# Six columns of zeros beside three products of a group

## Chip, cores and metric

One core of a Trainium2 chip runs the whole program. The metric is the device time of one execution in microseconds.

## The reference

A decoder trunk of two layers works on 16 meta tokens and 256 tokens with 2048 features in float32. Layer 0 is forgetting attention, layer 1 is stick-breaking attention on keys and values that have a projection of their own; each layer ends in an MLP with squared ReLU. Shortened:

```python
h = concatenate([meta, x])                                  # 272 x 2048
for layer in range(2):
    a = rms_norm(h, norm_attn[layer])
    if layer == 0:
        q, k, v, f = split(a @ fox_w_in)
        h = h + forgetting_attention(q, k, v, cumsum(log_sigmoid(f + b_f))) @ fox_w_o
    else:
        k, v = split(rms_norm(h, kv_norm) @ w_kv)
        h = h + stick_breaking_attention(a @ sb_w_q, k, v) @ sb_w_o
    m = rms_norm(h, norm_mlp[layer])
    h = h + square(relu(m @ w_up[layer])) @ w_down[layer]
return rms_norm(h, final_norm)[16:]
```

Only the last 256 tokens are returned. So in layer 1 the queries, the output projection and the MLP are computed for 256 tokens, the keys and values for 272.

## The kernel before

Everything is kept with the features on the partitions: `hT` holds the residual stream as 16 chunks of 128 features by 272 tokens. A matrix product with 2048 x 512 weights is a **group** (`gemm_group`). It makes four accumulators `acc` in PSUM (m = 0 to 3, 128 output features each) and runs over four blocks of weights (kb = 0 to 3) with four chunks of 128 input features each (kc).

The products run in the type fp32r with operands that are split in two. ScalarE rounds a weight tile `raw` to `whi` (line 222), VectorE forms the remainder `wlo` (line 223), and the inputs are split likewise into `hi` and `lo` of a `Split` tile. For each weight tile and chunk there are three products: whi with hi, whi with lo, and wlo with hi. A group therefore has 4 x 4 x 4 x 3 = 192 products of a 128x128 weight tile with 272 columns (layer 0, and the keys and values) or 256 columns (the rest of layer 1, `t0` = M = 16). Each product has its own weight load on TensorE. All of them are issued by the helper `gemm_matmul`, so the profile puts them on line 175, and the name of the input tile tells the stage: x_a for the normed input of the query, key and value projections of layer 0 and of the queries of layer 1, x_kv for the shared keys and values, x_o for the output projections, x_m for the MLP's up, x_u for its down projections.

The order of a block's products is fixed by `series`. For 256 columns:

```python
series = [(w, x, kc, m) for w, x in ((0, "hi"), (0, "lo"), (1, "hi")) for m in ms for kc in kcs]
```

In the first block, `ms` is one accumulator and `kcs` is all four chunks, so the first twelve products of a group are whi with hi for the chunks 0 to 3, whi with lo for the chunks 0 to 3, and wlo with hi for the chunks 0 to 3, all into accumulator 0. `gemm_matmul` also ties each product to the one before, so that the scheduler keeps this order.

Layer 1 has, in this order, 4 groups of the query projection (the norm's `finish` comes inside the first one, with two plain fp32 products `pms_a`, line 156), 8 groups of keys and values with the attention's own work between them, 4 groups of the output projection (`out_proj`), and the MLP: four times four up and four down groups. Inside the first up group, ahead of the third block, stands `finish` again (`pms_m`).

The `Split` tiles come from a pool with two buffers. A tile has 16 rows of 640 elements for each partition; with 256 tokens, hi takes the elements 0 to 255 of a row and lo takes 320 to 575, so 64 elements behind each are unused. The tile `pad` (128x32 zeros, written by POOL at the start) is not read by anything.

Of the kernel before, what the change touches and what calls it, by code (L numbers as in the profile page):

```python
# [15 lines left out]
P = 128  # L16
D = 2048
NC = D // P
M = 16
# [5 lines left out]
N_FF = 4  # L25

ROWS = {0: (48, 368), M: (0, 320)}
XROW = 640

G_A0, G_M0, G_KV, G_A1, G_M1, G_FIN = range(6)  # L30
# [3 lines left out]
def yoco_kernel(ctx: ExitStack, tc: tile.TileContext, hT_in, gains, b_f, w_f, w_qkv0, w_o0, w_up, w_dn,  # L34
                w_kv, w_q1, w_o1, outT):
    nc = tc.nc
# [77 lines left out]
    pad = align.tile([P, 32], F32, name="pad")  # L114
# [3 lines left out]
    class Split:  # L118


        def __init__(self, label, t0):
            n = T - t0
            self.t0 = t0
            rows = xs.tile([P, NC * XROW + 64], F32R, tag="x", name=f"x_{label}")
            hi, lo = ROWS[t0]
            o = min(hi, lo)
            rows = rows[:, o:o + NC * XROW].rearrange("p (c t) -> p c t", c=NC)
            self.hi, self.lo = (rows[:, :, k - o:k - o + n] for k in (hi, lo))

    def split_chunk(sp, gi, c):  # L130

        g = g_sb[:, gi, c:c + 1]
        nc.scalar.activation(sp.hi[:, c], hT[:, c, sp.t0:], AF.Copy, scale=g)
        nc.vector.scalar_tensor_tensor(out=sp.lo[:, c], in0=hT[:, c, sp.t0:], scalar=g,
                                       in1=sp.hi[:, c].bitcast(F32), op0=ALU.mult, op1=ALU.subtract)
# [37 lines left out]
    def gemm_matmul(*args, **kw):  # L173

        ins = nc.tensor.matmul(*args, **kw).ins  # L175
        if queued and pinned[0]:
            tc.add_manual_dep(ins, queued[0].name, mybir.DependencyInfo(mybir.DependencyClass.NoSync,
                                                                        mybir.DependencyReason.DATA))
        queued[:] = [ins]

    def gemm_group(wblk, sp, t0, evac, before={}, after={}, load_x=None):

        uid[0] += 1
        u = uid[0]
        accs = [pacc.tile([P, 512], F32, tag="acc", name=f"acc_{u}_{m}") for m in range(4)]
        n = T - t0  # L190
        for kb in range(4):
            src_w = wblk[kb].rearrange("p (k c) -> p k c", k=4)
            if kb in before:
                before[kb]()
            piece = 1 if load_x is not None and kb < 2 else 2
            raws = [wraw.tile([P, 2, 512], F32, tag="raw", name=f"raw_{u}_{kb}_{hf}") for hf in range(2)]
            for k0 in range(0, 4, piece):
                if load_x is not None:
                    load_x(range(4 * kb + k0, 4 * kb + k0 + piece))
                if load_x is not None and kb == k0 == 0:  # L200

                    for c0 in (0, 256):
                        nc.scalar.dma_start(raws[0][:, 0, c0:c0 + 256], src_w[:, 0, c0:c0 + 256])
                else:
                    nc.sync.dma_start(raws[k0 // 2][:, k0 % 2:k0 % 2 + piece], src_w[:, k0:k0 + piece])
            parts = []
            for hf in range(2):
                whi = wspl.tile([P, 2 * 576], F32R, tag="whi", name=f"whi_{u}_{kb}_{hf}")
                wlo = wspl.tile([P, 2, 576], F32R, tag="wlo", name=f"wlo_{u}_{kb}_{hf}")
                if t0:  # L210
                    whi = whi.rearrange("p (k c) -> p k c", k=2)[:, :, 16:528]
                    wlo = wlo[:, :, 16:528]
                else:
                    whi = whi[:, :1024].rearrange("p (k c) -> p k c", k=2)
                    wlo = wlo[:, :, :512]
                boxes = [(o, piece, 0, 512) for o in range(0, 2, piece)]
                if load_x is not None and kb == hf == 0:
                    boxes[:1] = [(0, 1, 0, 256), (0, 1, 256, 512)]
                for o, no, c0, c1 in boxes:
                    src = raws[hf][:, o:o + no, c0:c1]  # L220
                    hp, lp = whi[:, o:o + no, c0:c1], wlo[:, o:o + no, c0:c1]
                    on_act = nc.scalar.activation(hp, src, AF.Copy)  # L222
                    on_dve = nc.vector.tensor_tensor(out=lp, in0=src, in1=hp.bitcast(F32), op=ALU.subtract)  # L223
                parts.append((whi, wlo))
            if kb in after:
                with tc.issue_after(on_act.ins), tc.issue_after(on_dve.ins):
                    after[kb]()


            if load_x is not None and kb == 0:  # L230
                runs = [([kc], range(4)) for kc in range(4)]
            elif kb in (0, 3):
                runs = [(range(4), [m]) for m in range(4)]
            else:
                runs = [(range(2 * hf, 2 * hf + 2), range(4)) for hf in range(2)]
            pinned[0] = load_x is None
            for kcs, ms in runs:
                if t0:
                    series = [(w, x, kc, m) for w, x in ((0, "hi"), (0, "lo"), (1, "hi")) for m in ms for kc in kcs]
                else:  # L240
                    series = [(w, x, kc, m) for m in ms for kc in kcs for w, x in ((0, "hi"), (0, "lo"), (1, "hi"))]
                for w, x, kc, m in series:
                    gemm_matmul(accs[m][:, :n], parts[kc // 2][w][:, kc % 2, m * P:(m + 1) * P],
                                getattr(sp, x)[:, 4 * kb + kc], start=kb == kc == w == 0 and x == "hi", stop=kb == kc == 3 and w == 1)
                if kb == 3:
                    for m in ms:
                        evac(m, accs[m][:, :n])
# [101 lines left out]
    ao = Split("o0", 0)  # L349
    for g in range(4):  # L350
# [11 lines left out]
        if g == 0:  # L362

            gemm_group(w_qkv0[0], xa, 0, lambda m, acc, qT=qT: nc.scalar.copy(qT[:, m, :], acc),
                       after={kb: (lambda kb=kb: first_norm(kb)) for kb in range(4)}, load_x=load_x)
# [11 lines left out]
        def decays(j):  # L377

            for i, (o, n) in enumerate(((0, 144), (144, T))):
# [5 lines left out]
                   after={j: (lambda j=j: decays(j)) for j in range(4)})  # L385
# [75 lines left out]
    def out_proj(w, ao, t0, gi, label):  # L461
        norm = Norm(label, t0)
        xm = Split(label, t0)
        for g in range(4):
            def evac(m, acc, g=g):
                c = 4 * g + m
                residual_add(c, acc, t0)
                split_chunk(xm, gi, c)
                norm.add(c)
            gemm_group(w[g], ao, t0, evac)  # L470
        return xm, norm

    def mlp(layer, xm, norm, t0, last_evac):
        box = {}

        def get_rstd():
            box["r"] = norm.finish()

        for f in range(N_FF):
            u = Split(f"u{layer}_{f}", t0)  # L480
            for g in range(4):
                def evac(m, acc, g=g):
                    c = 4 * g + m
                    r = tmp.tile([P, T], F32, tag="relu", name=f"relu_{layer}_{f}_{c}")
                    u2 = tmp.tile([P, T], F32, tag="u2", name=f"u2_{layer}_{f}_{c}")
                    nc.vector.scalar_tensor_tensor(out=r[:, t0:], in0=acc, scalar=0.0, in1=box["r"][:, t0:],
                                                   op0=ALU.max, op1=ALU.mult)
                    nc.scalar.activation(u2[:, t0:], r[:, t0:], AF.Square)
                    nc.scalar.activation(u.hi[:, c], u2[:, t0:], AF.Copy)
                    nc.vector.tensor_tensor(out=u.lo[:, c], in0=u2[:, t0:], in1=u.hi[:, c].bitcast(F32),  # L490
                                            op=ALU.subtract)
                gemm_group(w_up[layer, f, g], xm, t0, evac, {2: get_rstd} if f == g == 0 else {})
            for g in range(4):
                def evac(m, acc, g=g):
                    residual_add(4 * g + m, acc, t0)
                    if f == N_FF - 1:
                        last_evac(4 * g + m)
                gemm_group(w_dn[layer, f, g], u, t0, evac)

    xm, norm_m = out_proj(w_o0, ao, 0, G_M0, "m0")  # L500


# [16 lines left out]
    for g in range(4):  # L519
        def evac_q1(m, acc, g=g):  # L520
            q = qT1[g][:, m, :S]
            nc.vector.scalar_tensor_tensor(out=q, in0=acc, scalar=QSCALE, in1=box["rstd"][:, M:],
                                           op0=ALU.mult, op1=ALU.mult)
        def split_c(kb, g=g):
            for c in ([4 * kb + g - 1] if g < 3 else [4 * kb + 2, 4 * kb + 3]):
                split_chunk(xc, G_KV, c)

        gemm_group(w_q1[g], xq, M, evac_q1, {2: get_rstd1} if g == 0 else {},
                   after={kb: (lambda kb=kb: split_c(kb)) for kb in range(4)} if g else {})

    ao = Split("o1", M)
    for g in range(4):
# [80 lines left out]
    xm, norm_m = out_proj(w_o1, ao, M, G_M1, "m1")  # L613
# [36 lines left out]
    for i in range(2):  # L650
        pr = patt.tile([P, 512], F32, tag="patt", name=f"pr_fin_{i}")
        for b in range(2):
            nc.tensor.matmul(pr[:, b * P:(b + 1) * P], rs[:, b:b + 1].to_broadcast([P, P]), ident,
                             start=True, stop=True)
# [67 lines left out]
```

## Time and profile before

| what | value |
|---|---|
| median of three runs | 2330.26 us (2329.82 to 2330.46) |
| the profiled execution | 2329.83 us |
| its span, first to last instruction | 2328.0 us |
| TensorE busy | 2316.8 us |
| VectorE, ScalarE busy | 1289.9 us, 1040.6 us |
| POOL busy | 38.4 us |
| read from HBM | 407.29 MB |

PE is TensorE's products, PEld its weight loads, DVE is VectorE, ACT is ScalarE, POOL is GpSimd, and SP issues most DMAs. TensorE's products are pipelined: one is listed with more than twice the time after which the next one starts. So its busy time and the mean time of one product don't tell the rate; a stretch's length over its count of products does. A row of groups reads: line, engine, operation, tile written <- tiles read, shape, count | busy us, mean ns of one | idle time before them and who ended it. A piece of the chain that ended last reads: start in us, length in us, engine, tile, line, count.

### The profile page before, as it was taken

The numbers are of one execution on the slowest core, as the hardware profiler recorded it, in microseconds if no ns is written. First come the engines' busy times: TensorE is split into PE (matmuls) and PEld (weight loads), VectorE is DVE, ScalarE is ACT, GpSimd is POOL, SyncE is SP. The second block draws the span as 40 slices with busy tenths as digits, with TensorE's granted clock in tenths as the row PEclk, the third lists the DMA queues.
The fourth block names the chain that finished last, engine by engine and source line by source line (L and its number), as shares of the span: only waits on it lengthen the run. The fifth ranks groups of instructions, "written<-read, shape, count | busy, mean of one in ns | idle before, by whom it ended". The sixth has DMA issues, their size and how long they took to land.

```text
span 2328.0 us, 44800 instructions
## 1 busy us (share of the span) xinstructions
PE 2316.8 (100%) x19030; PEld 2309.8 (99%) x19030; DVE 1289.9 (55%) x1764; ACT 1040.6 (45%) x1397; POOL 38.4 (2%) x58
## 2 busy tenths in 40 slices
PE   9999999999999999999999999999999999999998
PEld 9999999999999999999999999999999999999998
DVE  7656556554455455455565555566555555555554
ACT  6444344443353344344544444455534434443553
POOL 1000000000000000000000000000000000000000
PEclk9999999999999999999999999999999999999999
DMA  7444545555555555555555444456565655656563
GB/s 240 166 163 157 181 154 168 185 174 180 181 170 185 172 184 177 183 170 184 173 188 183 156 153 149 152 180 199 180 192 178 194 182 184 195 182 191 179 192 127
DMA packets 116904, 412.32 MB, mean 177 GB/s; under 512 B 13520, under 2 KB 16992, under 8 KB 116704
## 3 DMA queue, kind: packets, MB, share of 16 engines
q1 hardware_dynamic: 114560, 406.29, 53.7%
q8 instruction: 149, 2.44, 0.4%
q10 hardware_dynamic: 2144, 3.17, 0.4%
q14 instruction: 51, 0.42, 0.1%
HBM read 407.29 MB, written 2.11 MB: 176 GB/s over the span
## 4 chain that ended last, share of the span: by engine, by line
PE 99%; DVE 0%; DMA 0%; ACT 0%; SPq 0%; issue 0%; DVEq 0%; ACTq 0%
PE acc L175 96%; PE ps L392 0%; PE pv L325 0%; PE pza L569 0%; PE po L454 0%; PE po L608 0%; DMA raw<-w_qkv 0%; PE po L609 0%; PE pzb L570 0%; PE po L455 0%; DVE ob L664 0%; PE pf L291 0%; PE pf L292 0%; PE pta L584 0%; PE pta L585 0%; PE pp L424 0%
## 5 line engine op out<-in xcount | busy, mean ns | idle before, releaser
L223 DVE TENSOR_TENSOR wlo<-raw,whi 128x1024 fp32r<-128x1024 f32 (+1 forms) x773 | 928.7, 1217 | 761.5 <-ACT whi L222 759.8
L222 ACT ACTIVATE whi<-raw 128x1024 fp32r<-128x1024 f32 (+1 forms) x773 | 796.5, 1049 | 1034.2 <-PE acc L175 1006.5
L175 PE MATMUL acc<-x_u,whi 128*128 128x272 f32 (+1 forms) x4096 | 651.9, 284 | 0.0
L175 PE MATMUL acc<-x_m,whi 128*128 128x272 f32 (+1 forms) x4096 | 651.7, 284 | 0.0
L175 PEld LDWEIGHTS acc<-x_u,whi 128*128 128x128 f32 x4096 | 573.9, 189 | 0.0
L175 PEld LDWEIGHTS acc<-x_m,whi 128*128 128x128 f32 x4096 | 573.6, 189 | 0.1
L175 PE MATMUL acc<-x_u,wlo 128*128 128x272 f32 (+1 forms) x2048 | 445.3, 284 | 0.0
L175 PE MATMUL acc<-x_m,wlo 128*128 128x272 f32 (+1 forms) x2048 | 445.2, 284 | 0.0
L175 PE MATMUL acc<-x_a,whi 128*128 128x272 f32 (+1 forms) x2048 | 361.8, 289 | 0.1
L175 PEld LDWEIGHTS acc<-x_u,wlo 128*128 128x128 f32 x2048 | 327.6, 189 | 0.0
L175 PEld LDWEIGHTS acc<-x_m,wlo 128*128 128x128 f32 x2048 | 327.5, 189 | 0.0
L175 PEld LDWEIGHTS acc<-x_a,whi 128*128 128x128 f32 x2048 | 303.4, 189 | 1.4 <-ACT whi L222 0.4
L175 PE MATMUL acc<-x_a,wlo 128*128 128x272 f32 (+1 forms) x1024 | 254.8, 287 | 0.0
L175 PE MATMUL acc<-x_kv,whi 128*128 128x272 f32 x1024 | 191.8, 288 | 0.0
L175 PEld LDWEIGHTS acc<-x_a,wlo 128*128 128x128 f32 x1024 | 176.5, 189 | 0.9 <-issue 0.5
L175 PE MATMUL acc<-x_o,whi 128*128 128x272 f32 (+1 forms) x1024 | 161.9, 282 | 0.0
L175 PEld LDWEIGHTS acc<-x_kv,whi 128*128 128x128 f32 x1024 | 159.7, 188 | 0.0
L175 PE MATMUL acc<-x_kv,wlo 128*128 128x272 f32 x512 | 147.5, 288 | 0.0
L175 PEld LDWEIGHTS acc<-x_o,whi 128*128 128x128 f32 x1024 | 141.7, 188 | 0.0
L250 DVE TENSOR_TENSOR hT<-acc,hT 128x272 f32<-128x272 f32 (+1 forms) x160 | 69.0, 431 | 88.1 <-PE acc L175 86.9
L175 PE MATMUL acc<-x_o,wlo 128*128 128x272 f32 (+1 forms) x512 | 110.5, 282 | 0.0
L175 PEld LDWEIGHTS acc<-x_kv,wlo 128*128 128x128 f32 x512 | 96.5, 188 | 0.0
(221 smaller groups left out, 969.2 us busy)
## 6 DMA issues: line engine op xcount, KB each, us to landing
raw<-w_up SPq DMA_DIRECT2D x256, 512.0 KB, 4.5
raw<-w_dn SPq DMA_DIRECT2D x256, 512.0 KB, 4.5
raw<-w_qkv SPq DMA_DIRECT2D x92, 512.0 KB, 3.8
raw<-w_o SPq DMA_DIRECT2D x64, 512.0 KB, 4.4
raw<-w_kv SPq DMA_DIRECT2D x64, 512.0 KB, 3.8
raw<-w_q SPq DMA_DIRECT2D x32, 512.0 KB, 4.5
fk<-f_dram ACTq DMA_DIRECT2D x4, 544.0 KB, 5.0
raw<-w_qkv SPq DMA_DIRECT2D x7, 256.0 KB, 4.5
```

The source lines that it names most:

```text
L175: ins = nc.tensor.matmul(*args, **kw).ins
L222: on_act = nc.scalar.activation(hp, src, AF.Copy)
L223: on_dve = nc.vector.tensor_tensor(out=lp, in0=src, in1=hp.bitcast(F32), op=ALU.subtract)
L250: nc.vector.tensor_tensor(out=hT[:, c, t0:], in0=acc, in1=hT[:, c, t0:], op=ALU.add)
```

## The change

In chosen groups of layer 1, the products 0, 4 and 8 of the first block are 262 columns wide in place of 256. These are the ones that read chunk 0. The six additional columns are zeros which POOL copies from `pad` behind hi and behind lo of chunk 0, whenever a `Split` tile for 256 tokens is made; their products go to the columns 256 to 261 of accumulator 0, which nobody reads. The chosen groups are the last three of the query projection, all four of the output projection, and the second and the fourth of each four up and each four down groups of the MLP.

```diff
+SPAN = 6
...
+            if t0:
+                self.wide = {}
+                for name, k in (("hi", hi), ("lo", lo)):
+                    nc.gpsimd.tensor_copy(rows[:, 0, k - o + n:k - o + n + SPAN], pad[:, :SPAN])
+                    self.wide[name] = rows[:, 0, k - o:k - o + n + SPAN]
...
-    def gemm_group(wblk, sp, t0, evac, before={}, after={}, load_x=None):
+    def gemm_group(wblk, sp, t0, evac, before={}, after={}, load_x=None, widen=False):
...
-                for w, x, kc, m in series:
-                    gemm_matmul(accs[m][:, :n], parts[kc // 2][w][:, kc % 2, m * P:(m + 1) * P],
-                                getattr(sp, x)[:, 4 * kb + kc], start=kb == kc == w == 0 and x == "hi", stop=kb == kc == 3 and w == 1)
+                for i, (w, x, kc, m) in enumerate(series):
+                    over = SPAN if widen and kb == m == 0 and i in (0, 4, 8) else 0
+                    rhs = sp.wide[x] if over else getattr(sp, x)[:, 4 * kb + kc]
+                    gemm_matmul(accs[m][:, :n + over], parts[kc // 2][w][:, kc % 2, m * P:(m + 1) * P], rhs,
+                                start=kb == kc == w == 0 and x == "hi", stop=kb == kc == 3 and w == 1)
...
-            gemm_group(w[g], ao, t0, evac)
+            gemm_group(w[g], ao, t0, evac, widen=t0 == M)
...
-                gemm_group(w_up[layer, f, g], xm, t0, evac, {2: get_rstd} if f == g == 0 else {})
+                gemm_group(w_up[layer, f, g], xm, t0, evac, {2: get_rstd} if f == g == 0 else {},
+                           widen=t0 == M and g % 2 == 1)
...
-                gemm_group(w_dn[layer, f, g], u, t0, evac)
+                gemm_group(w_dn[layer, f, g], u, t0, evac, widen=t0 == M and g % 2 == 1)
...
-                   after={kb: (lambda kb=kb: split_c(kb)) for kb in range(4)} if g else {})
+                   after={kb: (lambda kb=kb: split_c(kb)) for kb in range(4)} if g else {}, widen=g > 0)
```

TensorE's order before, from the end of the first up group of layer 1's MLP into the second one (x_m is the MLP's input; 128x256 is what a product writes; equal rows that follow each other are counted):

```order
L175 MATMUL acc_3_17895<-x_m_16818,wlo_3_1_18098 128x256 x2
L175 MATMUL acc_0_18173<-x_m_16818,whi_0_0_18181 128x256 x2
L175 MATMUL acc_0_18173<-x_m_16818,whi_0_1_18185 128x256 x2
L175 MATMUL acc_0_18173<-x_m_16818,whi_0_0_18181 128x256 x2
L175 MATMUL acc_0_18173<-x_m_16818,whi_0_1_18185 128x256 x2
L175 MATMUL acc_0_18173<-x_m_16818,wlo_0_0_18182 128x256 x2
L175 MATMUL acc_0_18173<-x_m_16818,wlo_0_1_18186 128x256 x2
L175 MATMUL acc_1_18174<-x_m_16818,whi_0_0_18181 128x256 x2
```

The same place now (the numbers in the names and the line of the helper have shifted with the code):

```order
L182 MATMUL acc_3_17903<-x_m_16822,wlo_3_1_18106 128x256 x2
L182 MATMUL acc_0_18181<-x_m_16822,whi_0_0_18189 128x262
L182 MATMUL acc_0_18181<-x_m_16822,whi_0_0_18189 128x256
L182 MATMUL acc_0_18181<-x_m_16822,whi_0_1_18193 128x256 x2
L182 MATMUL acc_0_18181<-x_m_16822,whi_0_0_18189 128x262
L182 MATMUL acc_0_18181<-x_m_16822,whi_0_0_18189 128x256
L182 MATMUL acc_0_18181<-x_m_16822,whi_0_1_18193 128x256 x2
L182 MATMUL acc_0_18181<-x_m_16822,wlo_0_0_18190 128x262
L182 MATMUL acc_0_18181<-x_m_16822,wlo_0_0_18190 128x256
L182 MATMUL acc_0_18181<-x_m_16822,wlo_0_1_18194 128x256 x2
L182 MATMUL acc_1_18182<-x_m_16822,whi_0_0_18189 128x256 x2
```

No product has moved; the first, the fifth and the ninth of the group are 262 wide. VectorE, ScalarE and SP have the same instructions in the same order as before.

POOL's order before, from the first copy of layer 1's attention (pk_kc and pk_vc are the packed corners of keys and values) to the end:

```order
L334 COPY pk_kc_14616<-kT_0_14365 128x128
L334 COPY pk_vc_14943<-vT_0_14366 128x128
L334 COPY pk_kc_15229<-kT_1_14978 128x128
L334 COPY pk_vc_15556<-vT_1_14979 128x128
L334 COPY pk_kc_15842<-kT_2_15591 128x128
L334 COPY pk_vc_16169<-vT_2_15592 128x128
L334 COPY pk_kc_16455<-kT_3_16204 128x128
L334 COPY pk_vc_16782<-vT_3_16205 128x128
L668 TENSOR_TENSOR ob<-hT,pr_sb 128x2x256 x2
```

And now, the last of them:

```order
L343 COPY pk_kc_16459<-kT_3_16208 128x128
L134 CAST x_m_16822<-pad 128x6 x2
L343 COPY pk_vc_16786<-vT_3_16209 128x128
L134 CAST x_u_0_17897<-pad 128x6 x2
L134 CAST x_u_1_19977<-pad 128x6 x2
L134 CAST x_u_2_22044<-pad 128x6 x2
L134 CAST x_u_3_24111<-pad 128x6 x2
L678 TENSOR_TENSOR ob<-hT,pr_sb 128x2x256 x2
```

The pair for the MLP's input stands ahead of the last value corner; the four pairs for the hidden tiles u stand alone, and those of x_a and x_o (not shown) ahead of the first key corner.

## The prediction

> **What bounds the kernel now.** I read the page first, for the engine that never rests.
>
> ```profile
> span 2328.0 us, 44800 instructions
> PE 2316.8 (100%) x19030; PEld 2309.8 (99%) x19030; DVE 1289.9 (55%) x1764; ACT 1040.6 (45%) x1397; POOL 38.4 (2%) x58
> PEclk9999999999999999999999999999999999999999
> ```
>
> TensorE is busy all the time, at the full clock, and the others are half idle. The list of waits, asked for TensorE alone, says how much of that time it waits for somebody:
>
> ```profile
> PE pr_fin L653 <- DVE fin L647: 1.3, 1, 1.3
> PE idle L61 <- DVE mean_w L57: 1.1, 1, 1.1
> PE pms_fin L621 <- ACT sq_fin L633: 0.3, 1, 0.3
> ```
>
> That is 2.7 us, at the two ends of the program. In the middle only one thing can change the time: how far apart two products start. "Busy" hides that, because the products overlap (one is shown with some 280 ns). So I took the chain that ended last, whose pieces give a length and a count of products; the quotient is the step from one product to the next. First the pieces of the whole span, then of chosen stretches (start, length, what, count):
>
> ```profile
> 439.91 756.83 PE acc L175 x6144
> 1512.87 89.07 PE acc L175 x785
> 1602.36 708.08 PE acc L175 x6012
> ```
> ```profile
> 439.91 740.13 PE acc L175 x6001
> 1207.91 68.19 PE acc L175 x579
> 1545.94 44.09 PE acc L175 x389
> 1613.91 676.16 PE acc L175 x5741
> ```
>
> With 272 columns (layer 0) the step is 740.13/6001 = 123.33 ns. With 256 columns (layer 1) there are two steps. In the output projection it is 44.09/389 = 113.34 ns, which I call the quick step; in the query projection it is 68.19/579 = 117.77 and in the MLP 676.16/5741 = 117.78 ns, which I call the slow step. They differ by 4.44 ns, 3.9%, for products of the same shape, and neither leaves its step by itself: 5741 products in a row keep the slow one. Is it other work that makes the difference? The table by stretches, with columns span, PE, PEld, DVE, ACT and POOL busy, clock, DMA share and GB/s, holds the quick stretch against a slow one:
>
> ```profile
> 1546.00:1590.00 44.00, 44.00 (x391) 44.00 (x390) 28.84 (x42) 22.80 (x33) 0.00 (x0) 1.00 0.62 197
> 1614.00:1658.00 44.00, 44.00 (x376) 44.00 (x375) 24.74 (x32) 21.29 (x32) 0.00 (x0) 1.00 0.60 191
> ```
>
> Clock 1.00 in both, and VectorE, ScalarE and the DMA are busier in the quick one, so it isn't contention. It looks like two ways in which a stream of weight loads and products can lock. The evidence is where the stream passes from one to the other; short stretches of the chain show it:
>
> ```profile
> 1186.41 10.09 PE acc L175 x89
> 1196.73 0.46 PE pms_a L156 x2
> 1499.30 2.61 PE acc L175 x23
> 1508.19 3.18 PE acc L175 x27
> 1601.93 0.43 PE pms_m L156 x2
> 1602.36 10.13 PE acc L175 x86
> ```
>
> At 1186.41 (the first query group) the step is 113.4 and at 1499.30 (the first output group) 113.5 ns: both times the stream came straight from 272 columns to 256, with nothing between, and both times it fell into the quick step. At 1508.19 it is 117.8 ns, after transposes and other products of the attention; the piece of 785 from 1512.87 is quick again after another such break. At 1602.36 it is 117.8 ns, behind the two plain fp32 products of the norm, and stays so for the rest of the program. The norm of the query projection (pms_a) does the same: x_a is quick before it and slow at 1207.91, with the same tile read, so it isn't the buffers either. A break made of other instructions led to slow in three of four cases, a mere change of width led to quick in two of two.
>
> **The change part by part.**
>
> *The wider products themselves.* 3 + 4 + 16 = 23 groups with three each, 69 products. A column costs (123.33 − 117.78)/16 = 0.35 ns against the slow step and (123.33 − 113.34)/16 = 0.62 against the quick one, so six columns cost 2.1 to 3.7 ns and all 69 together 0.14 to 0.26 us. From above, a product of 262 may cost as much as one of 272, 10 ns, which makes 0.7 us; below nothing there is no reason, if the step of its neighbours is left out, which comes next. I take 0.4 us, since the lock has to be found again behind each. [...]
>
> *The step of what follows.* A wide product ends some 2 to 4 ns later than its neighbours would, in a stream that is otherwise unbroken. This is the nearest thing to the two changes of width that led to the quick step, and it comes three times in a row of nine, so at three different moments. The first wide product of the MLP is in the second group of the first up-projection. Of the 6012 products from 1602.36 on, 96 stand ahead of it; 5916 are behind. If all of them take the quick step, that is 5916 × 4.44 ns = 26.3 us. In the query projection the groups 1 to 3 hold 576 products, 2.6 us. The output projection is quick already and has nothing to win; whether the wide products disturb it is a rival below. I take it that they don't for long: the quick lock was reached from a jump of 16 columns twice, so it draws the stream in from some distance.
>
> *Who is late next.* Quicker products need the weights sooner. The quick stretch moved 197 GB/s and had no idle TensorE over 389 products, with more evacuation work than the MLP has; 191 GB/s × 117.78/113.34 = 198. So nothing new becomes late.
>
> *The zeros.* Fourteen copies of 128x6 on POOL, two for each of the seven operand tiles of 256 tokens. The nearest rows of POOL:
>
> ```profile
> L341 POOL COPY pk_sm<-s 128x64 f32<-128x64 f32 x8 | 2.7, 360 | 117.7 <-DVE s L402 87.1 <-PE pp L425 30.6
> L115 POOL MEMSET pad<- 128x32 f32 x1 | 0.1, 124 | 0.0
> ```
>
> So 0.12 to 0.36 us each. Each pair waits until its buffer is free, and behind it wait the later copies of POOL, the first product that reads the zeros, and ScalarE's first write of the same tile. The pairs for the u tiles run when the last down group of the chunk before is done; the first write comes a group (some 22 us) later, the first wide read five groups later. Only one pair stands ahead of something near: that of the MLP's input, ahead of the last copy of a value corner (pk_vc):
>
> ```profile
> L334 POOL COPY pk_vc<-vT x1: 1221/1221/1221, 1499.3 to 1499.3; 128x128 f32<-128x128 f32 x1
> L600 PE MATMUL pvc<-ident,pk_vc x1: 272/272/272, 1502.3 to 1502.3; 128*128 128x128 f32 x1
> ```
>
> The copy ends at 1500.5 and is read at 1502.3: 1.8 us of cover against at most 0.72. Cost nothing; without the cover at most 0.72 us, once.
>
> **Sum.** 26.3 + 2.6 − 0.4 = 28.5 us. The profiled execution took 2329.83 us, 1.83 more than its span; the median of the runs is 2330.26. From the median: 2301.8 us.
>
> **The rivals.**
>
> *The wide product changes nothing behind it.* The slow lock takes the stream back within a few products. For it: 5741 products held it, through groups, waits for weights and chunk changes. Against: none of these was a change of width. Then 2330.26 + 0.4 = 2330.7 us. [...] Chance 0.13.
>
> *It only throws the stream out of the quick step.* The 785 quick products of the output projection and the first up group become slow, the rest stays: 785 × 4.44 ns = 3.5 us, with the 0.4 that is 2334.2. For it: each of the four output groups is hit, while quick. Chance 0.05.
>
> *Each hit draws anew.* Then the stream is quick about as often as after the six breaks above, three of six, over 6492 products: 14.4 us won, 1.7 us lost in the output projection, 0.4 paid: 2318.0; if only one time in three is quick, 2323.4. Chance 0.13.
>
> *A third step, slower than both.* Nothing says that 256 columns lock in only two ways. If the wide products lead to one of, say, 120 ns, between the slow one and that of 272 columns, the 6492 products lose 2.2 ns each and the 785 quick ones 6.7: 14.4 + 5.2 = 19.6 us, 2349.9. With the step of 272 columns it would be 36.0 + 7.8 us, 2374. It decides from an average of 0.7 ns above the slow step, which makes 4.7 us. Against it: all long stretches of 256 have one of two values. Chance 0.08.
>
> **How the numbers follow.** The forecast has 0.61. About 0.2%, 4.7 us, is what a measurement of this kernel can tell from no change. Faster by more: the forecast and the redraw, 0.74. Within: the first two rivals, 0.18, for 2334.2 is 0.17% over. Slower: the third step, 0.08. The range starts at 2300.0, if the wide products cost nothing and some breaks fall better, and reaches to 2331.0, so that it holds the forecast, the redraw and the case of no effect, 0.87 together; narrower, it would have to leave one of these out and fall to 0.74. The forecast's own range is 2300 to 2306, with the first two or three hit groups of the MLP missed (384 products, 1.7 us, a pair).
>
> **What would show it.** In the chain after, the long piece behind the norm of the MLP should split in the time of its products: 117.8 ns for the first up group's rest and 113.4 from the second group on, to the end; the query projection likewise from its second group. Groups of TensorE products should show 276 ns where x_u and x_m show 281 now. The waits of TensorE should stay at 2.7 us. I am wrong if the MLP keeps 117.8 ns (then the lock isn't moved by six columns), if it alternates from pair to pair of groups (redraw), if a step above 117.8 shows, or if the output projection has lost its 113.3.

## The result, and the profile after

The changed kernel takes 2302.31 us (median of four runs, 2301.95 to 2303.47), the kernel before 2330.36 beside it (median of four, 2329.82 to 2331.12). The ratio is 0.988, with a 95% interval of 0.9863 to 0.9897: 28.0 us less.

The page of the changed kernel, and the list of waits for TensorE alone:

```profile
span 2301.7 us, 44826 instructions
PE 2290.6 (100%) x19030; PEld 2282.9 (99%) x19030; DVE 1289.2 (56%) x1764; ACT 1041.2 (45%) x1397; POOL 41.5 (2%) x72
```
```profile
PE pr_fin L663 <- DVE fin L657: 1.3, 1, 1.3
PE idle L62 <- DVE mean_w L58: 1.1, 1, 1.1
PE acc L182 <- ACT whi L229: 0.3, 1, 0.3
PE pms_fin L631 <- ACT sq_fin L643: 0.3, 1, 0.3
```

TensorE does the same 19030 products and still waits for almost nothing. The only new wait is 0.3 us, on a weight tile, in the first 60 us of the program. What has changed is the step, the time from the start of one product to the start of the next. The chain that ended last, first of the kernel before (the one piece that the prediction didn't show: the end of the query projection and the beginning of keys and values), then of the changed kernel:

```profile
1197.19 106.54 PE acc L175 x894
```
```profile
441.21 756.83 PE acc L182 x6144
1198.49 104.08 PE acc L182 x894
1511.73 89.13 PE acc L182 x785
1601.29 682.16 PE acc L182 x6012
```

Piece by piece, with the same counts: the query projection's is 2.46 us shorter, the output projection's 0.06 longer, the MLP's 25.92 shorter. Layer 0's is the same to the hundredth. Together 28.32 us. Two stretches of the changed kernel's chain, in the query projection and in the MLP, give the steps:

```profile
1210.99 63.07 PE acc L182 x556
1613.90 656.17 PE acc L182 x5787
```

That is 113.44 and 113.39 ns, the quick step with the wide products' price in it. The starts of single products in the trace show the passage: from the first wide product on, some thirteen steps run from 122 down to 114 ns, and then the quick step holds to the end, in the query projection from its second group on, in the MLP from the second up group on. The products of x_m and x_u with 256 columns, shown with 281 ns before, are shown with 276 now. The table by stretches shows the same 44 us of the MLP as before:

```profile
1614.00:1658.00 44.00, 44.00 (x391) 44.00 (x390) 25.56 (x34) 22.91 (x34) 0.00 (x0) 1.00 0.60 192
```

Where 376 products started before, 391 do now.

The profiled execution took 2303.47 us and its span is only 26.3 us shorter. Nearly all of the rest lies at the ends: layer 0's long piece starts at 441.21 in place of 439.91, 1.30 us later, in an execution whose loads began more slowly (5.70 MB in the first 20 us in place of 6.13), and the last four products of the program took 1.24 us in place of 0.72 (both are taken up at the end).

### The profile page after: what moved, and what is told of

Read it like the earlier page. It is cut to its first block, busy times and chain, and to the rows that moved or that the text cites. A ratio compares the mean times of both kernels' runs of the same rounds, so it can differ in the third digit from the quotient of the medians.

```text
span 2301.7 us, 44826 instructions
## 1 busy us (share of the span) xinstructions
PE 2290.6 (100%) x19030; PEld 2282.9 (99%) x19030; DVE 1289.2 (56%) x1764; ACT 1041.2 (45%) x1397; POOL 41.5 (2%) x72
## 4 chain that ended last, share of the span: by engine, by line
PE 99%; DMA 1%; DVE 0%; ACT 0%; issue 0%; DVEq 0%; SPq 0%; ACTq 0%
PE acc L182 95%; DMA raw<-w_qkv 1%; PE ps L401 0%; PE pv L334 0%; PE pza L579 0%; PE po L463 0%; PE po L618 0%; PE pzb L580 0%; PE po L619 0%; PE po L464 0%; DMA hT<-hT_in 0%; DVE ob L674 0%; PE pf L301 0%; PE pf L300 0%; PE pta L594 0%; PE pta L595 0%
## 5 line engine op out<-in xcount | busy, mean ns | idle before, releaser
L182 PE MATMUL acc<-x_m,whi 128*128 128x272 f32 (+1 forms) x4096 | 643.2, 281 | 0.0
L182 PE MATMUL acc<-x_u,whi 128*128 128x272 f32 (+1 forms) x4096 | 642.9, 281 | 0.0
L182 PEld LDWEIGHTS acc<-x_m,whi 128*128 128x128 f32 x4096 | 566.1, 188 | 0.1
L182 PEld LDWEIGHTS acc<-x_u,whi 128*128 128x128 f32 x4096 | 565.9, 188 | 0.0
```

## The experiments

A single time stands for one execution; the kernel before took 2329.85 to 2330.66 us beside these. The verdicts rest on the pieces of the chain. A "hit" group is one with wide products.

**Only POOL's copies.** No product is wide; the copies and the waits on them stay.

```diff
-                    over = SPAN if widen and kb == m == 0 and i in (0, 4, 8) else 0
+                    over = SPAN if widen and kb == m == 0 and i in () else 0
```

> All products stay 256 wide; only POOL's fourteen copies of zeros and the waits on them are left of the change. Theory (the wide products move the stream into the quick step): nothing is gained, 2330.3 us within 0.7, the MLP keeps 117.8 ns a product. Rival (the copies or their waits on TensorE move the stream): about 2302 us, the MLP at 113.3 ns from its second up group on.

Measured 2330.19 us beside 2329.85. The chain has the slow step in the query projection and the MLP, as before:

```profile
1196.93 106.53 PE acc L182 x894
1602.10 708.08 PE acc L182 x6012
```

So the copies and their waits neither move the stream nor cost anything that shows.

**Two groups in place of 23.** Three wide products in the second query group and in the second up group of the first quarter of the MLP, none elsewhere.

```diff
-            gemm_group(w[g], ao, t0, evac, widen=t0 == M)
+            gemm_group(w[g], ao, t0, evac)
...
-                           widen=t0 == M and g % 2 == 1)
+                           widen=t0 == M and f == 0 and g == 1)
...
-                gemm_group(w_dn[layer, f, g], u, t0, evac, widen=t0 == M and g % 2 == 1)
+                gemm_group(w_dn[layer, f, g], u, t0, evac)
...
-                   ..., widen=g > 0)
+                   ..., widen=g == 1)
```

> Three wide products in only two groups: the second of the query projection and the second up group of the MLP. Theory (a lock that holds once it is reached): the query projection and the MLP are quick from there to the end as in the changed kernel, and 20 ns are saved in each of 21 groups, 0.4 us: about 2301.7 us. Rival (the wide products have to come again and again): the step falls back to 117.8 ns somewhere; if behind the next group, the gain is under 2 us, 2328 us or more.

Measured 2302.30 us. The chain:

```profile
1197.74 104.04 PE acc L182 x894
1510.92 89.07 PE acc L182 x785
1600.42 681.86 PE acc L182 x6012
```

The quick step holds through the rest of the MLP with nothing to renew it, over some 5900 products. The MLP's piece is 0.30 us shorter than in the changed kernel, for 15 hit groups less: 20 ns a group, 6.7 ns for each wide product that meets a quick stream. The single steps of the changed kernel agree: behind such a product they are 116, 116, 114 and 114 ns, together 6.7 ns over four quick ones, and then the quick step is back. The whole time is no shorter than the changed kernel's median. This execution began late too (its piece of the query projection starts at 1197.74, that of the kernel before at 1197.19).

**One wide product, with none, one or two more products ahead.** In these two groups only the first product is wide. In two further kernels one or two additional products of 256 columns stand ahead of it, so that it falls on the next place of whatever rhythm the slow step has.

```diff
-... i in (0, 4, 8) else 0
+... i == 0 else 0
...
+                for _ in range(1 if widen and kb == 0 and ms[0] == 0 else 0):      # 2 in the last kernel
+                    gemm_matmul(accs[0][:, 256:512], parts[0][0][:, 0, :P], sp.hi[:, 0], start=True, stop=True)
                 for i, (w, x, kc, m) in enumerate(series):
```

> As the run with two hit groups, but only the first product of the group is wide, not the fifth and the ninth. Theory, with the moment mattering: one wide product takes the stream out of the slow step only at some of three moments; in the changed kernel the stream was quick only behind the third, so this one alone leaves the slow step in force or changes to quick after a few products, with even chances: 2330.3 or 2301.7 us, the query projection and the MLP alike, since both are hit at the same place of the slow rhythm. Rival (any wide product is enough): 2301.7 us here and with one or two additional products ahead. Rival (three in a row are needed): 2330.3 us in all of these.

> As the run with a single wide product in each of two groups, with one additional product of 256 columns ahead of it, whose result nobody reads; so the wide one comes one product later in the rhythm of the slow step. Theory, with the moment mattering: among none, one and two additional products at least one takes the stream into the quick step and at least one does not. Rival (any wide product is enough): quick in all three, 2301.7 to 2302 us. Rival (three are needed): 2330.5 us in all three.

> The single wide product in each of two groups, with two additional products of 256 columns ahead. With none and with one additional product the stream became quick. Theory as it stands now (any wide product in a slow stream is enough, at whatever moment of the rhythm): quick again, from the second query group and the second up group on, 2300.8 to 2302.5 us. Rival (one of the three moments fails): the MLP stays at 117.8 ns, 2330.5 us.

Measured 2300.73, 2302.31 and 2302.20 us. The MLP's piece in the three:

```profile
1599.40 681.82 PE acc L182 x6012
```
```profile
1600.39 681.92 PE acc L182 x6013
```
```profile
1600.12 682.04 PE acc L182 x6014
```

All three are quick. My theory, that the moment matters and at least one of the three places fails, fell: one wide product is enough at each of them. The second and the third of the change are not needed to win the quick step, and they put it off: by the single steps, the MLP's stream is quick five products after the start of the single wide one, and some thirteen after the first of three. With one the piece is 0.04 us shorter than with three. Of the 1.6 us between the first two totals only 0.1 lies in the MLP's piece (the additional product), and the rest ahead of it and behind it (the piece starts at 1599.40 and 1600.39).

**An additional product, nothing wide.** One more product of 256 columns at the start of the same two groups.

> One additional product of 256 columns at the start of the same two groups, and nothing wide. Theory (the width is what moves the stream): slow throughout, 2330 to 2331 us. Rival (any irregularity at a group's start is enough): quick, about 2302 us.

Measured 2329.55 us beside 2330.66; the MLP's piece:

```profile
1602.03 708.20 PE acc L182 x6013
```

Slow throughout. One more product of the same width does nothing; in the runs above it is the six columns that move the stream.

**Other widths.** The single wide product two or sixteen columns wider (`SPAN = 2`, `SPAN = 16`).

> The single wide product in each of the two groups, two columns wider in place of six. Theory (any later end moves the stream out of the slow step): quick, 2300.8 to 2302.5 us. Rival (the slow step takes up small delays, some three columns or more are needed): the MLP stays at 117.8 ns, 2330.3 us. Even chances.

> The single wide product in each of the two groups, sixteen columns wider, so of the width of layer 0. Theory: quick, as behind the two changes from 272 to 256 columns in the kernel before, 2300.8 to 2302.5 us. Rival (the step's rhythm comes back after a delay of 16 columns, 6.67 ns at 2.4 columns a ns, of which 53 make three slow steps): slow, 2330.3 us. I hold the first for more likely, three to one.

Two columns: 2302.40 us. Sixteen: 2330.81. The pieces:

```profile
1197.93 104.00 PE acc L182 x894
1600.57 681.82 PE acc L182 x6012
```
```profile
1197.62 106.54 PE acc L182 x894
1602.80 708.08 PE acc L182 x6012
```

Two columns are as good as six. Sixteen change nothing, in both places, and here I had held the other outcome for likelier. The single steps show how: the step behind the wide product is 124 ns in the MLP and 125 in the query projection, about 6.7 more than a slow step; the next steps are 116 and 115, and then the slow step goes on, all within 117 to 119. It was tempting to see a beat in it: 17 x 6.667 ns is the quick step, 53 x 6.667 ns are three slow ones, 37 x 6.667 ns are two of 272 columns, and 16 columns delay by about one such beat. So the next kernel put two widths against that.

**Thirty-two and twenty-two columns.** One wide product in each of the two groups.

```diff
-SPAN = 6
+SPAN = 32
...
+                    over = (SPAN if after else 22) if widen and kb == m == 0 and i == 0 else 0      # after: the query projection
-                    rhs = sp.wide[x] if over else getattr(sp, x)[:, 4 * kb + kc]
+                    rhs = sp.wide[x][:, :n + over] if over else getattr(sp, x)[:, 4 * kb + kc]
```

> A single wide product in each of the two groups, of two widths in one kernel: 32 columns more in the second group of the query projection, 22 more in the second up group of the MLP. Theory from the run with 16 columns (the steps keep to a beat of 6.67 ns, the time of 16 columns at 2.4 columns a ns, and a delay of whole beats leaves the slow step in force): 32 columns are two beats, the query projection stays at 117.8 ns; 22 are one beat and six columns, the MLP becomes quick; 2330.3 - 26.2 = about 2304 us. Rival (16 columns failed for being too many): both stay slow, 2330.3 us. Second rival (16 was a single unlucky case): both become quick, 2301 to 2302.5 us.

Measured 2301.96 us:

```profile
1197.49 104.01 PE acc L182 x894
1600.13 681.82 PE acc L182 x6012
```

Both are quick, so 32 columns are not two idle beats, and the theory of the beat fell in this form. The steps themselves speak against whole beats too: in the slow stretch of the kernel before (1613.91 to 2290.07) every single one lies between 117 and 119 ns, so the slow step is not a mixture of 17 and 18 beats (113.3 and 120.0 ns). Of five additions, 2, 6, 22 and 32 columns move the stream and 16 don't; 32 were tried in the query projection alone and 22 in the MLP alone. Why 16 fail stays open.

**The wide products in layer 0.** Every second group of 272 columns, from the second on, has its first three products 278 wide.

```diff
-            if t0:
+            if True:
...
-                    over = SPAN if widen and kb == m == 0 and i in (0, 4, 8) else 0
+                    over = SPAN if (widen or not t0 and load_x is None and u % 2 == 0) and kb == m == 0 and (kc == 0) else 0
```

> As the changed kernel, and in every second group of 272 columns (from the second on) the three products of chunk 0 and accumulator 0 are 278 wide. Question: is the 123.33 ns of 272 columns a slow step too, with a quicker one beside it (120.0 ns, 3.33 ns less, for which single steps in the trace speak)? Theory (two locks exist at this width too): layer 0's 32 groups of the MLP would fall to 120.0 ns, 6144 x 3.33 ns = 20 us, about 2282 us. Rival (272 columns have one lock): each hit costs some 3 to 10 ns and the step comes back, 28 x 3 x 3 to 10 ns: 0.3 to 0.8 us more, 2302.6 to 2303.1 us. I hold the rival for likelier, four to one, since the stream of 272 columns had many breaks and always came back to 123.33.

Measured 2302.83 us. A stretch of layer 0 and its long piece:

```profile
599.90 580.15 PE acc L182 x4702
439.98 757.13 PE acc L182 x6144
```

123.38 ns in the stretch; the long piece is 0.30 us longer than in the changed kernel, for 16 hit groups. The stream comes back to 123.33 ns each time. Six columns find no quicker step at 272 columns. The single steps of 120 ns that the expectation names are not in layer 0's part of the long piece of the kernel before, where all but one lie between 122 and 125.

**Behind the norm, once.** The slow step begins at the norm inside the first query group and the first up group, so the wide product went there: the ninth behind the norm. The first product of the same group must be wide too, to open the six columns of the accumulator.

```diff
-                for name, k in (("hi", hi), ("lo", lo)):
+                for name, k, c in (("hi", hi, 0), ("lo", lo, 8)):
...
-                    over = SPAN if widen and kb == m == 0 and i in (0, 4, 8) else 0
+                    over = SPAN if widen and m == 0 and (kb == i == 0 or kb == 2 and kc == 0 and x == "lo") else 0
...
-                           widen=t0 == M and g % 2 == 1)
+                           widen=t0 == M and f == g == 0)
...
-                   ..., widen=g > 0)
+                   ..., widen=g == 0)
```

> One wide product, six columns, as the ninth product behind the norm, in the first query group and in the first up group of the MLP, where the slow step begins; its six columns of accumulator 0 are opened by the first product of the same group, which is wide too and meets a quick stream; no other product is wide. Theory (one wide product is enough, wherever the slow stream is met): the slow step ends some 90 products earlier than in the changed kernel, 2 x 88 x 4.44 ns = 0.8 us, and 23 x 20 ns less are paid for wide products, 0.4 us: 1.2 us below the changed kernel, about 2301.0 us. Rival (so near to the norm the stream isn't caught): the slow step stays to the end, as nothing comes later to take it out: 2330.3 us.

> The changed kernel itself, beside the one that hits once behind each norm: 2302.3 us; by the theory 1.2 us above the other, by the rival 28 us below it.

Measured 2300.71 us (2299.79 to 2302.32), ratio to the kernel before 0.9874 with the interval 0.9857 to 0.989; the changed kernel beside it 2302.32 us, ratio 0.988 (0.9865 to 0.9895). The chain of the kernel that hits behind the norm:

```profile
1197.01 103.60 PE acc L182 x894
1509.75 89.07 PE acc L182 x785
1599.26 681.42 PE acc L182 x6012
```

Against the changed kernel's pieces that is 0.48 + 0.06 + 0.74 = 1.28 us less, where 1.2 were expected. The medians differ by 1.6 us, but the two intervals overlap, so the pieces carry this verdict and not the times. It has the shortest pieces of all versions here.

## Why the prediction was right

*That the step between products bounds the kernel.* Right: the waits of TensorE stayed at 3.0 us, and the pieces of the chain make up 28.32 us, where the times differ by 28.0.

*That the two steps are two states of one stream, and neither contention nor buffers.* Right: with the same instructions and tiles, but for one wide product in each of two groups, the run with one hit in the MLP differs from that with the copies alone by 26.26 us in 6012 products (708.08 and 681.82), and 5916 x 4.44 ns are 26.27.

*That a change of width leads to quick.* Right for the change, in both places. The rule was drawn from two transitions from 272 to 256 columns, and it was too general: a single product of 272 columns between products of 256 did nothing. The forecast had luck in that six isn't sixteen. The reason I gave for three wide products, three different moments, was no reason: one did it at each of three places, and the second and the third only put it off.

*That the quick stream stands the wide products.* Right: the output projection's piece grew by 0.06 us, and the quick step came back behind every hit. *The price:* I had 2.1 to 3.7 ns by the column and 10 at most; in a quick stream it is 6.7 ns, 69 of them 0.46 us, where I took 0.4. The total came out near, though the price of one was nearly double the range by the column.

*The zeros.* The copies of 128x6 took 0.19 us each, inside the bounds, and the last value corner is still early (its copy and its reader in the changed kernel):

```profile
L134 POOL CAST x_m<-pad 128x6 fp32r<-128x6 f32 x2 | 0.3, 190 | 26.5 <-PE acc L182 26.5
L343 POOL COPY pk_vc<-vT x1: 1150/1150/1150, 1498.2 to 1498.2; 128x128 f32<-128x128 f32 x1
L610 PE MATMUL pvc<-ident,pk_vc x1: 272/272/272, 1501.2 to 1501.2; 128*128 128x128 f32 x1
```

The copy ends at 1499.4, 1.8 us ahead of its reader, as before.

*The rivals.* No effect behind the wide product: excluded for six columns, true for sixteen. Quick thrown out by a hit: excluded, the output projection kept its step. A new draw at each hit: excluded, for no later hit lost the quick step, and without a hit 5900 products kept it too. A third step: no lasting one was seen at 256 columns in thirteen kernels.

*What stays open.* Which part of TensorE keeps the step, and why 16 columns leave it alone. No run here shows the mechanism; the runs show only which disturbances change the state.

## What to carry to other kernels

Where one engine is busy to 100% and waits for nobody, divide the length of a stretch by its count of instructions, stage by stage: two values for one shape can be a gain that the busy shares hide, as here. If a short break (here two products of another kind) sets the slow value, look for the smallest disturbance that ends it, place it right behind the break, and test that it holds with nothing to renew it. Try several sizes of it: one that fails, as the 16 columns here, says little about the others.

## What I had not expected

Two columns more in a single product, one of 6012, make the MLP 26 us faster.

The two ends of the program scatter by more than the small terms of this study. The last four products (pr_fin) took 0.72 us in one execution and 1.24 in another, whatever the step was: the pieces are of the kernel before, of the run with the copies alone (slow too) and of the run with one wide product.

```profile
2318.51 0.72 PE pr_fin L653 x4
```
```profile
2318.25 1.24 PE pr_fin L663 x4
```
```profile
2289.29 0.72 PE pr_fin L663 x4
```

Together with the start of the program, after which layer 0's long piece began anywhere from 439.45 to 441.21 us, this is why terms under 2 us had to be read from the chain's pieces.
